# A two-layer decoder trunk: weight loads on ScalarE's DMA queue with three raw buffers, and longer PSUM rings by stage

## The chip, the cores and the metric

The kernel runs on one core of one Trainium2 chip. The metric is the device time in microseconds (us) of one execution of the whole program; lower is better. The core has TensorE (PE, matrix products, results in the banks of PSUM), VectorE (DVE), ScalarE (ACT), GpSimd (POOL) and SyncE (SP), each with its own instruction stream that it works off strictly in order. DMA transfers are issued by an instruction in one of these streams; a DMA instruction that has to wait holds up whatever stands behind it in that stream.

## The reference, cut to what matters

The program is one inference step of a decoder trunk of two layers on 512 prompt tokens and 8 single decode tokens (T = 520 columns). Layer 0 mixes tokens with a gated delta rule (GDN), layer 1 with a Mamba-2 scan (SSD); a gated convolutional feed-forward follows each.

```python
def _conv_ffn(x, buf, w_up, conv_w, conv_b, w_down):
    gv = x @ w_up
    gate, val = gv[..., :D_FF], gv[..., D_FF:]
    gate, new_buf = _causal_dwconv(gate, buf, conv_w, conv_b)
    return (jax.nn.silu(gate) * val) @ w_down, new_buf
...
        if i % N_MIXERS == 0:
            h, nb, ns = _gdn_mixer(...)   # proj, conv, chunked delta rule, gated norm, @ w_out
        else:
            h, nb, ns = _ssd_mixer(...)   # proj, conv, chunked scan, gated norm, @ w_out
        x = _layer_norm(DN_ALPHA * x + h, ln1_g[i], ln1_b[i])
        f, fb = _conv_ffn(x, ffn_conv[i], ffn_w_up[i], ffn_conv_w[i], ffn_conv_b[i], ffn_w_down[i])
        x = _layer_norm(DN_ALPHA * x + f, ln2_g[i], ln2_b[i])
```

D_MODEL is 1024, D_FF 2816. Besides the tokens the outputs hold the new convolution caches and the new states of the mixers: the 8 decode tokens each read, update and write back a state per head, which is most of the DMA traffic that isn't weights.

## The kernel before

Features lie on the 128 partitions, tokens on the free axis, in two halves of HT = 260 columns. All projections are cut into **units**: one block of 128 output features, in one or both halves. There are 252 units and 294 weight **chunks** of up to 8x128x128 float32 values (512 KB). The order of the units is a list (`plan`, L132): the GDN input projection (`gin`), its output projection (`gout`), feed-forward `up0` and `down0`, then `sdt` and `sin`, `sout`, `up1`, `down1`.

**A chunk.** `prep` (L209) takes a tile `raw` (tag "raw", 2 buffers), loads it by a DMA on SP's queue (L215), casts it on ACT to a rounded copy `hi` (L223), and subtracts on DVE or POOL to get the rest `lo` (L224). `hi` and `lo` have 3 buffers each. In `gin` and part of `sin` the subtraction runs on POOL, elsewhere on DVE. `raw` is free for the next chunk when both L223 and L224 are through.

**A unit.** `unit` (L228) takes a PSUM bank per half from `unit_bank` (L117), calls `prep` until two chunks beyond its own are prepared, and for each k of 8 issues three matmuls of 260 columns, hi by XH, hi by XL, lo by XH (L246; `XH`, `XL` are the split activations). Then `evac` empties the bank: in `gin` and `sin` a copy on ACT to `u` (L587, in the program's names `u<-psl`), in `up` a copy on ACT to `u` (L428 for the first half, L442 for the second) for the 22 gate units and a product on DVE to `f` (L481) for the 22 value units, in the output projections a sum on DVE (`R` or `lR`, L308). `f` has 3 buffers, and is split by ACT into `fh` (L278) and by POOL into `fl` (L279).

**Banks.** PSUM has eight banks. In the GDN stage (`self.scan` true) the units turn through the two banks of tag "l"; the other six (A, B, C, D, X, Y) belong to the small matmuls of the chunked delta rule. In every later stage the units turn through three: X, l, l.

**The state updates.** `state` (L978) is called for the decode states, two at a time, from the evacuations of the gate units: an SP load of `Sd` (L984), an SP load of `Sr` (L987), three operations on POOL (L988, L989, L990), and an SP store (L991) that waits for the last of these. `Sd` and `Sr` have 2 buffers. In `up0` there are 16 such updates, in `up1` 32.

**The delta rule.** Per head, `gdn_head` (L736) builds what the chunked rule needs (`kt`, `Kd`, the solve `D`, `X`, `Z`), and `gdn_chunk` (L885) walks the recurrence. The gate units of `gin` (m of 24 and more) write to `z`, a tile of tag "uh" with 2 buffers.

**What sets the order.** The Tile framework's scheduler fixes one order per engine when the program is built, from the order of the code, priorities (`high_priority` around the chunk's load and split) and when buffers come free. On the chip each engine runs its own list in order and waits on semaphores.

Of the kernel before, what the change touches and what calls it, by code (L numbers as in the profile page):

```python
# [9 lines left out]
F32 = mybir.dt.float32  # L10
# [3 lines left out]
ALU = mybir.AluOpType  # L14
# [4 lines left out]
P = 128  # L19
# [3 lines left out]
B = 8  # L23
T = S + B
HT = T // 2
C = 4
# [13 lines left out]
KB = 3  # L40
FF = 2816
# [28 lines left out]
def _bc(ap, dims):  # L70
    return ap.to_broadcast(dims)


class Net:
    def __init__(self, ctx, tc, a):
        self.tc, self.nc, self.a, self.ctx = tc, tc.nc, a, ctx
        nc = self.nc
        pool = lambda name, bufs=1, **k: ctx.enter_context(tc.tile_pool(name=name, bufs=bufs, **k))
        self.const = pool("const")
        self.wp = pool("wp", 3)  # L80
        self.big = pool("big")
# [8 lines left out]
        self.odd, self.scanodd, self.scan, self.nb, self.na = False, False, True, 0, 0  # L90
        self.plan()

    def consts(self):
        nc, a, p = self.nc, self.a, self.const
# [5 lines left out]
        self.halves = p.tile([P, 2, B], F32, name="halves")  # L100
        nc.vector.memset(self.halves[:, 0], -0.5)
        nc.vector.memset(self.halves[:, 1], 0.5)
# [29 lines left out]
    def plan(self):  # L132
# [23 lines left out]
        self.prepped = 0  # L156
# [51 lines left out]

    def prep(self):  # L209
        name, m, k0, kn, i = self.chunks[self.prepped]  # L210
        nc = self.nc
        mw = 64 if name in ("w_gba", "w_sdt") else P
        with self.tc.high_priority():
            raw = self.wp.tile([P, 8, P], F32, tag="raw", name="raw", bufs=2)
            nc.sync.dma_start(out=raw.rearrange("p k m -> p (k m)")[:, :kn * mw], in_=self.a[name][m][:, k0 * mw:(k0 + kn) * mw])  # L215
            raw = raw.rearrange("p k m -> p (k m)")[:, :kn * mw].rearrange("p (k m) -> p k m", m=mw)
# [234 lines left out]
    def ffn(self, l):  # L451
        nc, tc, a = self.nc, self.tc, self.a
        W = 3
        with tc.tile_pool(name=f"ffn{l}", bufs=1) as fp:
            fh = fp.tile([P, KF, T], F32R, name="fh")
            fl = fp.tile([P, KF, T], F32R, name="fl")
            with tc.tile_pool(name=f"up{l}", bufs=1) as p:
# [25 lines left out]

                while self.next_name() == f"up{l}":
                    self.unit(evac)
                nc.sync.dma_start(out=a["o_fconv"][:, l], in_=cout)
# [27 lines left out]
    def softplus(self, pool, z, n, tag):  # L514

        nc = self.nc
        t = {k: pool.tile([P, n], F32, tag=tag + k, name=tag + k) for k in "ewqr"}
        e, w, q, r = (t[k] for k in "ewqr")
# [40 lines left out]
    def gdn(self):  # L559
        nc, tc, a = self.nc, self.tc, self.a  # L560
        W = 4
        with tc.tile_pool(name="gdnr", bufs=1) as rp:
# [6 lines left out]
            with tc.tile_pool(name="gdn", bufs=1) as p:  # L569
# [59 lines left out]
                self.scan = False  # L629
# [106 lines left out]
    def gdn_head(self, p, h, kq, v, decays):  # L736
# [9 lines left out]
        Kd = p.tile([P, C, P], F32, tag="Kd", name="Kd", bufs=4)  # L746
# [54 lines left out]
        tmp = p.tile([P, 2, C, 16], F32, tag="Xtmp", name="Xtmp", bufs=2)  # L801
# [207 lines left out]
    def ssd(self):  # L1009
        nc, tc, a = self.nc, self.tc, self.a  # L1010
        W = 4
        with tc.tile_pool(name="ssdr", bufs=1) as rp:
# [4 lines left out]
            with tc.tile_pool(name="ssd", bufs=1) as p:  # L1017
# [35 lines left out]

                while self.next_name() in ("sdt", "sin"):
                    self.unit(evac)
                nc.sync.dma_start(out=a["o_sconv"], in_=cout)
# [193 lines left out]
    def ssd_norm(self, p, g):  # L1250
# [11 lines left out]
        f = p.tile([P, T], F32, tag="nf", name="nf", bufs=1)  # L1262
# [176 lines left out]
```

## Time and profile before

| | us |
|---|---|
| three runs before | 1784.18, 1792.85, 1791.64 (median 1791.64) |
| the profiled execution: its own time | 1785.41 |
| its span, first to last instruction | 1783.6 |
| PE busy | 1613.7 (90%) |
| DVE busy | 1221.2 (68%) |
| POOL busy | 968.4 (54%) |
| ACT busy | 839.3 (47%) |
| mean granted TensorE clock | 0.973 |

The stages, read from the first matmul of each: `gin` 5 to 384 us, `gout` to 443, `up0` to 723, `down0` to 858.6, the SSD stage (`sdt`, `sin`) to 1238.3, `sout` to 1351, `up1` to 1637, `down1` to 1772, the last layer norm to 1783.6.

A busy PE is a PE with a matmul in its pipeline: successive matmuls of 260 columns overlap, so that a row has 0.28 us although one starts every 0.12 us. What a stage loses is therefore read from the number of matmuls in it against its length. Waits are listed as "who <- whom: total us, times, longest us"; a queue (SPq) is the stream of DMA-issuing instructions of an engine.

### The profile page before, as it was taken

To read this page: it belongs to the slowest core of one execution; us is meant where nothing else is said; L and a number is where in the kernel's file an instruction comes from. 1 tells how busy PE (TensorE), PEld (TensorE's weight loads), DVE (VectorE), ACT (ScalarE), POOL (GpSimd) and SP (SyncE) were. 2 spreads that over 40 slices of the span, in tenths; PEclk is the share of its full clock that TensorE was granted. 3 is DMA by queue.
4 is the path that set the end of the run, shared out by engine and by line. 5 is a ranking of instruction groups with operands and counts; after the bars stand their busy time and mean duration, and the time that the engine had idled before them with its cause. 6 is when DMAs were issued, how large, how long until landed. Compare 5 with 4: busy or idle time off the path is not lost.

```text
span 1783.6 us, 33737 instructions
## 1 busy us (share of the span) xinstructions
PE 1613.7 (90%) x12889; PEld 1550.4 (87%) x12889; DVE 1221.2 (68%) x2133; ACT 839.3 (47%) x1724; POOL 968.4 (54%) x1090
## 2 busy tenths in 40 slices
PE   8888899888999899999888897989988998889997
PEld 7888888888998799998886796979988998889996
DVE  5967888668876544337699989895569765554356
ACT  4644664354563344225665554645236643333134
POOL 4844677655258722215346757676134387876142
PEclk9989999999999999999999999989999999999999
DMA  5422343235466532334644534342564655564334
GB/s 187 131 85 61 103 130 111 86 122 163 146 204 196 171 116 96 88 97 131 188 129 153 163 119 130 125 125 70 160 197 143 209 198 187 190 210 153 96 101 145
DMA packets 108978, 250.36 MB, mean 140 GB/s; under 512 B 15344, under 2 KB 31696, under 8 KB 108784
## 3 DMA queue, kind: packets, MB, share of 16 engines
q1 hardware_dynamic: 108816, 248.20, 44.1%
q8 instruction: 101, 1.65, 0.4%
q14 instruction: 61, 0.50, 0.1%
HBM read 225.80 MB, written 22.92 MB: 139 GB/s over the span
## 4 chain that ended last, share of the span: by engine, by line
PE 30%; DVE 24%; DMA 18%; POOL 14%; ACT 8%; issue 5%; SPq 1%; ACTq 0%; DVEq 0%; POOLq 0%
PE psl L246 26%; DVE lo L224 3%; DMA raw<-w_up 3%; DMA Sr<-bd 3%; POOL Sd L990 3%; ACT hi L223 3%; POOL Sr L988 3%; DVE sE L1180 2%; DMA Sr<-kr 2%; DVE y L419 2%; DMA raw<-w_down 2%; POOL Sd L989 2%; POOL fl L279 1%; DVE Xtmp L812 1%; DMA Sd<-sstate 1%
## 5 line engine op out<-in xcount | busy, mean ns | idle before, releaser
L246 PE MATMUL psl<-XH,hi 128*128 128x260 f32 (+1 forms) x2816 | 819.5, 292 | 61.4 <-ACT u L442 18.4
L246 PE MATMUL psl<-XL,hi 128*128 128x260 f32 (+1 forms) x2848 | 823.6, 290 | 8.8 <-DVE lR L308 3.9
L246 PE MATMUL psl<-XH,lo 128*128 128x260 f32 (+1 forms) x2816 | 809.7, 288 | 2.7 <-DVE lo L224 1.6
L246 PEld LDWEIGHTS psl<-XH,hi 128*128 128x128 f32 (+1 forms) x2816 | 538.9, 192 | 78.0 <-ACT u L442 22.0
L224 DVE TENSOR_TENSOR lo<-raw,hi 128x512 fp32r<-128x512 f32 (+2 forms) x439 | 356.9, 850 | 327.7 <-ACT hi L223 323.3
L246 PEld LDWEIGHTS psl<-XL,hi 128*128 128x128 f32 (+1 forms) x2848 | 545.6, 192 | 15.4 <-issue 5.7
L246 PEld LDWEIGHTS psl<-XH,lo 128*128 128x128 f32 (+1 forms) x2816 | 539.2, 192 | 7.6 <-DVE lo L224 3.1
L223 ACT CAST hi<-raw 128x512 fp32r<-128x512 f32 (+2 forms) x499 | 315.2, 671 | 435.0 <-PE psl L246 191.7
L246 PE MATMUL psl<-fh,lo 128*128 128x260 f32 x704 | 201.2, 286 | 1.8 <-DVE lo L224 1.4
L246 PE MATMUL psl<-fh,hi 128*128 128x260 f32 x704 | 200.3, 284 | 0.7 <-ACT hi L223 0.7
L246 PE MATMUL psl<-fl,hi 128*128 128x260 f32 x704 | 198.8, 282 | 0.0
L224 POOL TENSOR_TENSOR lo<-raw,hi 128x1024 fp32r<-128x1024 f32 x60 | 148.6, 2476 | 53.5 <-ACT hi L223 52.1
L246 PEld LDWEIGHTS psl<-fh,lo 128*128 128x128 f32 x704 | 132.5, 188 | 4.0 <-DVE lo L224 3.6
L246 PEld LDWEIGHTS psl<-fh,hi 128*128 128x128 f32 x704 | 132.5, 188 | 1.4 <-ACT hi L223 0.9
L246 PEld LDWEIGHTS psl<-fl,hi 128*128 128x128 f32 x704 | 132.4, 188 | 0.2
L279 POOL TENSOR_TENSOR fl<-f,fh 128x260 fp32r<-128x260 f32 x88 | 80.3, 914 | 66.4 <-ACT fh L278 66.3
L419 DVE SCALAR_TENSOR_TENSOR s<-u,par,s 128x512 f32<-128x512 f32 x88 | 82.6, 939 | 6.8 <-ACT s L416 6.8
L278 ACT CAST fh<-f 128x260 fp32r<-128x260 f32 x88 | 36.0, 409 | 96.5 <-DVE f L481 96.5
L246 PE MATMUL psl<-y,hi 128*128 128x260 f32 x256 | 73.3, 288 | 1.8 <-DVE y L279 0.8
L990 POOL TENSOR_TENSOR Sd<-Sd,Sr 128x512 f32<-128x512 f32 x48 | 70.1, 1460 | 0.5
L365 POOL TENSOR_TENSOR lnsq<-lnsq,sq 128x260 f32<-128x260 f32 x48 | 46.8, 978 | 28.8 <-ACT sq L363 27.3
L471 POOL COPY cout<-u 128x10 f32<-128x10 f32 x44 | 19.2, 436 | 77.7 <-ACT u L442 77.6
(397 smaller groups left out, 2685.9 us busy)
## 6 DMA issues: line engine op xcount, KB each, us to landing
raw<-w_up SPq DMA_DIRECT2D x106, 512.0 KB
raw<-w_down SPq DMA_DIRECT2D x44, 512.0 KB
raw<-w_sin SPq DMA_DIRECT2D x43, 512.0 KB
raw<-w_gin SPq DMA_DIRECT2D x32, 512.0 KB
Sd<-sstate SPq DMA_DIRECT2D x64, 256.0 KB
raw<-w_down SPq DMA_DIRECT2D x22, 384.0 KB
Sd<-gstate SPq DMA_DIRECT2D x32, 256.0 KB
kb<-kr SPq DMA_DIRECT2D x32, 256.0 KB
```

What stands on the lines that cost most here:

```text
L223: nc.scalar.copy(out=hi[:, ks, :mw], in_=raw[:, ks, :])
L224: eng.tensor_tensor(out=lo[:, ks, :mw], in0=raw[:, ks, :], in1=hi[:, ks, :mw].bitcast(F32), op=ALU.subtract)
L246: self.nc.tensor.matmul(out=ps[h][:mw], lhsT=w[:, b0 + k, :mw], rhs=x[:, hs], start=(k0 + k == first and i == 0), stop=(k0 + k == last and ...
L278: nc.scalar.copy(out=hi, in_=xf)
L279: (eng or nc.gpsimd).tensor_tensor(out=lo, in0=xf, in1=hi.bitcast(F32), op=ALU.subtract)
L365: nc.gpsimd.tensor_tensor(out=acc, in0=acc, in1=sq, op=ALU.add)
L419: nc.vector.scalar_tensor_tensor(out=y[:, :S], in0=u[:, j:j + S], scalar=self.pcol(wname, i * w + j), in1=y[:, :S], op0=ALU.mult, op1=ALU.add)
L471: nc.gpsimd.tensor_copy(out=cout[:, m, :], in_=u[:, 2 + S - 2:2 + T])
L988: nc.gpsimd.tensor_tensor(out=t, in0=t, in1=_bc(col[:, :, None], D4), op=ALU.mult)
L989: nc.gpsimd.tensor_tensor(out=St, in0=St, in1=_bc(decay[:, :, None], D4), op=ALU.mult)
L990: nc.gpsimd.tensor_tensor(out=St, in0=St, in1=t, op=ALU.add)
L1180: nc.vector.tensor_scalar(out=E[:, c, :], in0=E[:, c, :], scalar1=self.acum[:, c, h:h + 1], scalar2=0.0, op0=ALU.subtract, op1=ALU.min)
```

## The change

- `fetch` is new. It takes a `raw` tile (now `RAW` = 3 buffers) and issues its load on ScalarE's queue (`nc.scalar.dma_start`, L223 of the new file; the cast to `hi` is L241 there). `prep` calls it until the chunks up to two beyond the one it prepares are fetched. No weight load is left on SP.
- `unit_bank` turns through a ring that depends on the stage: two banks in the GDN stage (as before), three in the SSD stage (as before), six (X, l, A, Y, l, B) in `gout`, `down0`, `sout`, `down1`, and all eight in `up0` and `up1`.
- SBUF for the third `raw` buffer (4 KB a partition) comes from five places: `halves` has one column per value instead of a filled tile, and is broadcast in `power`; the residual tiles of the layer norms always use tag "u"; `softplus` reuses a tile; `Kd` has 3 buffers instead of 4; `Xtmp` 1 instead of 2; `nf` takes the place of `acc`.

```diff
+    BANKS = {"gdn": "ll", "ssd": "Xll", "out": "XlAYlB", "up": "XlAYlBCD"}
+
     def unit_bank(self):
         self.nb += 1
-        if not self.scan and self.nb % 3 == 1:
-            return self.pss.tile([P, 512], F32, tag="X", name="psl", bufs=1)[:, :HT]
-        return self.psl.tile([P, HT], F32, tag="l", name="psl")
+        tag = self.BANKS[self.stage][self.nb % len(self.BANKS[self.stage])]
+        if tag == "l":
+            return self.psl.tile([P, HT], F32, tag="l", name="psl")
+        return self.pss.tile([P, 512], F32, tag=tag, name="psl", bufs=1)[:, :HT]
...
-    def prep(self):
-        name, m, k0, kn, i = self.chunks[self.prepped]
-        nc = self.nc
+    def fetch(self):
+        name, m, k0, kn, i = self.chunks[self.fetched]
         mw = 64 if name in ("w_gba", "w_sdt") else P
         with self.tc.high_priority():
-            raw = self.wp.tile([P, 8, P], F32, tag="raw", name="raw", bufs=2)
-            nc.sync.dma_start(out=raw.rearrange("p k m -> p (k m)")[:, :kn * mw], in_=...)
-            raw = raw.rearrange("p k m -> p (k m)")[:, :kn * mw].rearrange("p (k m) -> p k m", m=mw)
+            raw = self.wp.tile([P, 8, P], F32, tag="raw", name="raw", bufs=RAW)
+            raw = raw.rearrange("p k m -> p (k m)")[:, :kn * mw]
+            self.nc.scalar.dma_start(out=raw, in_=...)
+        self.raws[self.fetched] = raw.rearrange("p (k m) -> p k m", m=mw)
+        self.fetched += 1
+
+    def prep(self):
+        while self.fetched < min(self.prepped + RAW, len(self.chunks)):
+            self.fetch()
+        ...
+        with self.tc.high_priority():
+            raw = self.raws.pop(self.prepped)
...
     def new_xr(self):
-        if self.lni % 2:
-            return self.lnp.tile([P, HT], F32, tag="xr", name="xr", bufs=4)
         return self.up.tile([P, 3 + T], F32, tag="u", name="xr")[:, :HT]
...
-        self.nc.gpsimd.tensor_tensor(out=y, in0=x, in1=self.halves[:, which, :n], op=ALU.pow)
+        self.nc.gpsimd.tensor_tensor(out=y, in0=x, in1=_bc(self.halves[:, which:which + 1], [P, n]), op=ALU.pow)
...
-        Kd = p.tile([P, C, P], F32, tag="Kd", name="Kd", bufs=4)
+        Kd = p.tile([P, C, P], F32, tag="Kd", name="Kd", bufs=3)
...
-        tmp = p.tile([P, 2, C, 16], F32, tag="Xtmp", name="Xtmp", bufs=2)
+        tmp = p.tile([P, 2, C, 16], F32, tag="Xtmp", name="Xtmp", bufs=1)
```

Three places of the built programs show what moves. The first is SP in the middle of `up1`, where the states are updated; before:

```order
L215 DMA raw<-w_up 128x1024
L984 DMA Sd<-sstate 128x512
L987 DMA Sr<-bd 128x512
L984 DMA Sd<-sstate 128x512
L215 DMA raw<-w_up 128x1024
L991 DMA o_sdec<-Sd 128x512
L987 DMA Sr<-bd 128x512
L991 DMA o_sdec<-Sd 128x512
L215 DMA raw<-w_up 128x1024
```

and after:

```order
L1005 DMA Sr<-bd 128x512
L1002 DMA Sd<-sstate 128x512
L1005 DMA Sr<-bd 128x512
L1002 DMA Sd<-sstate 128x512
L1009 DMA o_sdec<-Sd 128x512 x2
```

The weight loads that stood behind a state store are gone, and the state loads and stores are alone.

The second is ACT in the same stretch; before:

```order
L442 COPY u<-psl 128x260
L416 ACTIVATE s<-u,par 128x520
L278 CAST fh<-f 128x260
L470 ACTIVATE s<-s 128x520
L223 CAST hi<-raw 128x512 x2
L278 CAST fh<-f 128x260
L223 CAST hi<-raw 128x512 x2
```

and after (L458, L432, L296, L486, L241 are the same operations as L442, L416, L278, L470, L223 before; L223 is now the load):

```order
L458 COPY u<-psl 128x260
L432 ACTIVATE s<-u,par 128x520
L223 DMA raw<-w_up 128x1024
L296 CAST fh<-f 128x260
L486 ACTIVATE s<-s 128x520
L241 CAST hi<-raw 128x512 x2
L296 CAST fh<-f 128x260
L223 DMA raw<-w_up 128x1024
L241 CAST hi<-raw 128x512 x2
```

A load now stands one or two ACT instructions behind the cast of the chunk whose buffer it takes, and in front of the next copies; in `gin` and `sin` it stands three to six behind.

The third is PE late in the GDN stage, at the small 32x32 products of the solve (`z`, `xz`); before:

```order
L246 MATMUL psl<-XH,lo 128x260
L847 MATMUL z<-X,M 32x32 x8
L893 MATMUL st<-uo,Kd 128x128
L901 MATMUL o<-Sn,gbc 128x128
L902 MATMUL o<-uo,gbc 128x128
L762 MATMUL kqk<-kq 128x256 x2
L246 MATMUL psl<-XH,hi 128x260
L246 MATMUL psl<-XL,hi 128x260
```

and after, the head of a run that goes on to 27 groups of small matmuls with no unit matmul in between (`psl`); two further runs there have 33 and 21 groups, and the last one 9, where before the four runs have 6, 11, 18 and 9:

```order
L264 MATMUL psl<-XH,lo 128x260
L848 MATMUL z<-X,M 128x64 x4
L780 MATMUL kqk<-kq 128x256 x2
L853 MATMUL xz<-Z_320,XT 128x64 x4
L855 MATMUL xz<-XT,Z_320 128x64 x4
L780 MATMUL kqk<-kq 128x256 x2
L865 MATMUL z<-X,M 32x32 x8
L871 MATMUL xz<-XT,Z_321 32x32 x8
L874 MATMUL xz<-Z_321,XT 32x32 x4
L530 MATMUL qt<-cn,kq 128x128 x4
L881 MATMUL z_2694<-X,M 64x64 x4
L886 MATMUL x_2701<-XT,Z_2699 64x64 x4
```

The order of the units among themselves is the same; small matmuls of the later heads moved towards the end of the stage and stand closer together.

## Rows read from the trace of the kernel before

**Rows 1.** Page, sections 1 and 5: engines' busy time; POOL's subtraction.

```profile
PE 1613.7 (90%) x12889; PEld 1550.4 (87%) x12889; DVE 1221.2 (68%) x2133; ACT 839.3 (47%) x1724; POOL 968.4 (54%) x1090
...
L224 POOL TENSOR_TENSOR lo<-raw,hi 128x1024 fp32r<-128x1024 f32 x60 | 148.6, 2476 | 53.5 <-ACT hi L223 52.1
```

**Rows 2.** Stages: window, length; PE, PEld, DVE, ACT, POOL (counts); clock, DMA.

```profile
5.00:384.00 379.00, 335.45 (x2808) 317.97 (x2809) 282.35 (x647) 191.36 (x523) 239.89 (x277) 0.95 0.36 112
...
443.00:723.00 280.00, 263.45 (x2123) 258.83 (x2122) 170.91 (x259) 131.04 (x265) 135.15 (x177) 0.99 0.47 152
...
858.60:1238.30 379.70, 331.45 (x2501) 306.43 (x2500) 324.89 (x542) 210.47 (x317) 234.08 (x193) 0.96 0.42 134
1238.30:1351.00 112.70, 100.23 (x784) 96.72 (x783) 71.91 (x116) 46.09 (x88) 35.35 (x39) 0.99 0.51 160
1351.00:1637.00 286.00, 264.93 (x2126) 258.88 (x2126) 182.10 (x248) 127.46 (x258) 201.07 (x257) 0.99 0.59 192
```

**Rows 3.** Windows of 50 us, same columns: across down0's start, and in up1.

```profile
700.00:750.00 50.00, 50.00 (x419) 50.00 (x418) 16.26 (x29) 13.05 (x27) 12.78 (x15) 1.00 0.30 88
...
1550.00:1600.00 50.00, 45.29 (x371) 44.41 (x370) 27.58 (x35) 18.72 (x38) 41.88 (x54) 1.00 0.64 202
```

**Rows 4.** Waits in up1: TensorE's weight loads, then ACT's casts.

```profile
PEld psl L246 <- ACT u L442: 15.4, 12, 2.7
PEld psl L246 <- DVE f L481: 5.3, 7, 1.2
PEld psl L246 <- ACT u L428: 4.0, 5, 1.5
...
ACT hi L223 <- DMA raw<-w_up: 86.7, 34, 5.8
```

**Rows 5.** Waits in SP's queue: up1, then the GDN stage.

```profile
SPq L991 <- POOL Sd L990: 82.6, 20, 6.6
...
SPq L215 <- POOL cout L599: 51.5, 11, 8.7
```

**Rows 6.** Timeline in up1, 1477 to 1486 us: one late weight load.

```profile
1477.41 1.29 POOL L990 TENSOR_TENSOR Sd<-Sd,Sr 128x512 f32<-128x512 f32 x1
...
1478.73 0.34 SPq L991 DMA_DIRECT2D o_sdec<-Sd  x1
...
1479.18 0.36 SPq L215 DMA_DIRECT2D raw<-w_up  x1
...
1484.25 1.14 ACT L223 CAST hi<-raw 128x512 fp32r<-128x512 f32 x2 [4.27 <-DMA raw<-w_up]
...
1486.03 0.39 PE L246 MATMUL psl<-XH,hi 128*128 128x260 f32 x1 [1.33 <-ACT u L428]
```

**Rows 7.** Timeline of POOL in up1: a pair of state updates.

```profile
1506.37 1.72 POOL L990 TENSOR_TENSOR Sd<-Sd,Sr 128x512 f32<-128x512 f32 x1
...
1512.84 1.55 POOL L989 TENSOR_TENSOR Sd<-Sd,ddt 128x512 f32<-128x512 f32 x1 [2.07 <-DMA Sd<-sstate]
...
1520.05 1.72 POOL L990 TENSOR_TENSOR Sd<-Sd,Sr 128x512 f32<-128x512 f32 x1
```

**Rows 8.** Waits in up0: TensorE's weight loads.

```profile
PEld psl L246 <- DVE f L481: 5.1, 5, 2.1
PEld psl L246 <- DVE R L308: 5.1, 1, 5.1
PEld psl L246 <- ACT u L442: 4.8, 4, 2.2
PEld psl L246 <- ACT u L428: 3.8, 4, 1.7
```

**Rows 9.** Waits in sout: TensorE's matmuls.

```profile
PE psl L246 <- DVE lR L308: 3.9, 4, 1.5
```

**Rows 10.** GDN stage: a wait of TensorE; a run of 18 small groups.

```profile
PE xz L835 <- DVE Z L832: 3.3, 3, 1.5
...
363.89 0.67 PE L863 MATMUL z<-X,M 64*64 64x64 f32 x8
...
370.70 0.49 PE L893 MATMUL st<-uo,Kd 128*128 128x128 f32 x2 [0.62 <-DVE uo L891]
```

More of the change, by code (lines that the diff above doesn't have):

```diff
@@ L40 @@
 KB = 3
+RAW = 3
 FF = 2816
@@ L90, in __init__ @@
         self.odd, self.scanodd, self.scan, self.nb, self.na = False, False, True, 0, 0
+        self.stage = "gdn"
         self.plan()
@@ L99, in consts @@
         nc.sync.dma_start(out=self.par, in_=a["par"])
-        self.halves = p.tile([P, 2, B], F32, name="halves")
-        nc.vector.memset(self.halves[:, 0], -0.5)
-        nc.vector.memset(self.halves[:, 1], 0.5)
+        self.halves = p.tile([P, 2], F32, name="halves")
+        nc.vector.memset(self.halves[:, :1], -0.5)
+        nc.vector.memset(self.halves[:, 1:], 0.5)
         self.mean = p.tile([P, P], F32, name="mean")
@@ L155, in plan @@
         self.upos = 0
-        self.prepped = 0
+        self.prepped = self.fetched = 0
+        self.raws = {}
         self.ready = {}
@@ L207, in lo_pool @@
         return name in ("gin", "sin") and len(halves) == 2 and (name == "gin" or i % 4 != 3)
+    def fetch(self):
+        name, m, k0, kn, i = self.chunks[self.fetched]
+        mw = 64 if name in ("w_gba", "w_sdt") else P
+        with self.tc.high_priority():
+            raw = self.wp.tile([P, 8, P], F32, tag="raw", name="raw", bufs=RAW)
+            raw = raw.rearrange("p k m -> p (k m)")[:, :kn * mw]
+            self.nc.scalar.dma_start(out=raw, in_=self.a[name][m][:, k0 * mw:(k0 + kn) * mw])
+        self.raws[self.fetched] = raw.rearrange("p (k m) -> p k m", m=mw)
+        self.fetched += 1
     def prep(self):
+        while self.fetched < min(self.prepped + RAW, len(self.chunks)):
+            self.fetch()
         name, m, k0, kn, i = self.chunks[self.prepped]
@@ L213, in prep @@
         with self.tc.high_priority():
-            raw = self.wp.tile([P, 8, P], F32, tag="raw", name="raw", bufs=2)
-            nc.sync.dma_start(out=raw.rearrange("p k m -> p (k m)")[:, :kn * mw], in_=self.a[name][m][:, k0 * mw:(k0 + kn) * mw])
-            raw = raw.rearrange("p k m -> p (k m)")[:, :kn * mw].rearrange("p (k m) -> p k m", m=mw)
+            raw = self.raws.pop(self.prepped)
             hi = self.wp.tile([P, 8, P], F32R, tag="hi", name="hi")
@@ L482, in evac @@
                         self.split(f, fh[:, m, hs], fl[:, m, hs])
+                self.stage = "up"
                 while self.next_name() == f"up{l}":
                     self.unit(evac)
+                self.stage = "out"
                 nc.sync.dma_start(out=a["o_fconv"][:, l], in_=cout)
@@ L516, in softplus @@
         nc = self.nc
-        t = {k: pool.tile([P, n], F32, tag=tag + k, name=tag + k) for k in "ewqr"}
-        e, w, q, r = (t[k] for k in "ewqr")
+        t = {k: pool.tile([P, n], F32, tag=tag + k, name=tag + k) for k in "ewq"}
+        e, w, q, r = (t[k] for k in "ewqe")
         nc.vector.scalar_tensor_tensor(out=w, in0=z, scalar=-1.0, in1=z, op0=ALU.mult, op1=ALU.min)
@@ L628, in gdn @@
                 nc.sync.dma_start(out=a["o_gconv"], in_=cout)
-                self.scan = False
+                self.scan, self.stage = False, "out"
                 def first(name, m, h, ps):
@@ L1052, in evac @@
                             self.ssd_group(p, g, st["B"], st["C"])
+                self.stage = "ssd"
                 while self.next_name() in ("sdt", "sin"):
                     self.unit(evac)
+                self.stage = "out"
                 nc.sync.dma_start(out=a["o_sconv"], in_=cout)
@@ L1261, in ssd_norm @@
                 nc.gpsimd.tensor_tensor(out=acc, in0=acc, in1=sq, op=ALU.add)
-        f = p.tile([P, T], F32, tag="nf", name="nf", bufs=1)
+        f = acc
         for j in range(2):
```

## The prediction

> **What bounds the kernel now.** I read the engines' totals first: PE is busy 90% of the span and nothing else over 68% [rows 1], so a gain has to come out of the tenth in which PE stands, or out of work elsewhere that makes it stand. Then the stages. The pace of PE with nothing in its way is the window across the end of up0 and the start of down0: 419 matmuls in 50 us, 0.1193 us each [rows 3]. By that pace the 2123 matmuls of up0 take 253.3 us and the stage has 280, an excess of 26.7; up1 has 286 - 253.6 = 32.4, sout 112.7 - 93.5 = 19.2 [rows 2]. The granted clock is 0.99 in these, so the excess is waiting. The GDN stage (43.6 us without a PE row) and the SSD stage (48.3) also wait, but there the small matmuls of the recurrences depend on DVE, which is busy 324.9 of the 379.7 us of the SSD stage [rows 2]: that stage has a second floor close to its length.
>
> What the excess of up1 is: weight loads of TensorE wait for a bank, 15.4 us for the copies L442, 5.3 for f, 4.0 for L428, 24.7 together [rows 4]. Why the copies are late is seen on one case [rows 6]: POOL ends a state addition at 1478.70; the store behind it leaves SP at 1478.73; the weight load stands next in SP's queue and leaves at 1479.18; the data come 5 us later; ACT has stood for 4.27 us before the cast at 1484.25, and behind that cast, in ACT's order, stands the copy that frees the bank for which PE waits 1.33 us. ACT waits for weights 86.7 us in up1 in this manner, and SP's stores wait 82.6 us for POOL [rows 4, 5]. So before the change a chain runs from POOL's states through SP to the weights, to ACT, to the bank, to PE.
>
> **The change, term by term,** against the profiled execution's 1785.4 us (the median of the runs shown is 1791.6, 6 us higher; the runs spread over 8.7).
>
> *up1.* No load stands behind a store any more, and eight banks let PE go on over some 2.9 us for each half unit (24 matmuls) that an evacuation is late, against three before. The most to be had is the 24.7 us of bank waits [rows 4]. But a second pace lies under it. A gate unit and its value unit are 4 x 24 matmuls, 11.5 us, and bring two state updates to POOL; POOL has a pair every 13.7 us (L990 at 1506.37 and at 1520.05), and before one of its operations stands 2.07 us for the state's own load [rows 7]. In 1550 to 1600 it is better: PE makes 371 of 419, so a pair takes 11.5 / 0.885 = 12.9 us, and POOL is busy 41.9 of the 50 [rows 3]. POOL also makes fl, in its order behind the states; f has three buffers, fl frees one, and DVE's f frees the bank. So the states can still hold PE by way of f, once the eight banks are full. I take the pair at 12.9, the better stretch that the trace has, since SP will carry the states' loads alone: 16 pairs x 0.8 = 13. **-13**, between -24 (bank waits all gone) and -3 (pair stays at 13.7; only the run-ahead of the longer ring is left, once).
>
> *up0.* Only 8 pairs, and POOL is busy 135 of 280 us [rows 2], so it does not set the pace. Bank waits are 5.1 for f, 4.8 and 3.8 for the copies, 13.7 in all; the 5.1 for R (L308) is the layer norm at the seam and stays [rows 8]. **-12**, between -16 and -5.
>
> *gout, down0, sout, down1.* Six banks instead of three where DVE sums into R: in sout 3.9 us of waits for it [rows 9]; what else is in sout's excess is the chain of the layer norms, which the change doesn't touch. I allow half as much again for the other three: **-6**, between 0 and -10.
>
> *ScalarE's cost.* An issue holds SP 0.36 us [rows 6]; the trace of before has no weight load on ACT, so I take the same: 294 x 0.36 = 106 us more on an engine busy 839 of 1784 [rows 1]; 53 chunks in up1 are 19 us on 127 of 286 [rows 2]. That is covered. Not covered by itself is the wait: a load may leave when the subtraction of the chunk three before is done, and in ACT's order the evacuating copies stand behind it. Such a wait on ACT is bounded by nothing (subtraction long done) and by a whole subtraction, 2.48 us on POOL [rows 1]. In up the load stands one or two instructions behind the cast, so it will wait, but eight banks cover a copy that is 1 or 2 us late. In the GDN and SSD stages there are two and three banks as before, and the load stands three to six instructions behind; so I take it nearer to nothing there.
>
> *The SSD stage.* Same ring, DVE its floor. POOL subtracts 28 chunks here (60 less the 32 of gin): at worst 28 x 2.48 = 69 us of ACT standing, of which a fifth may reach DVE and PE; on the other side the loads no longer stand behind SP's other work. **+2**, between -8 and +15.
>
> *The GDN stage.* Loads are freed from SP's waits for POOL (51.5 us [rows 5]), but PE waits little for weights there, so that is worth a few us at most. Kd with 3 buffers instead of 4 holds back the next head: the order has its small matmuls later and denser, runs of 27, 33, 21 and 9 groups where before there are 6, 11, 18 and 9, 46 more without a unit matmul between them. What such a group costs beyond its work is bounded by two rows: in the run of 18 groups that begins at 363.89 the only idle time is 0.62 us, at 370.70, 0.03 a group, since two heads were interleaved; a bare hop over DVE (xz waiting for Z) is 3.3 / 3 = 1.1 us [rows 10]. 46 groups are 2 us by the one and 51 by the other. The run of 18 is the same sort of work at the same place, so I take nearest to it, with one bare hop at the head of each of the three longer runs (3.3) and a little for ACT's new waits in front of two banks: **+6**, between -10 and +30 as the stage's own part of the range.
>
> *The rest* (halves broadcast, tiles reused, Xtmp with one buffer, nf in acc) puts no instruction more on any engine; nothing waits for them but what is in these stages' bounds.
>
> Sum: -13 - 12 - 6 + 2 + 6 = -23, so 1785.4 - 23 = **1762 us**.
>
> **Rivals.**
> *A, slower: the dense runs are bare.* If the hops of the delta rule's tail cost 1.1 us in each of the 46 groups, the GDN stage is 51 longer instead of 6: 1762 + 45 = 1807. For it speaks that the runs now hold steps of one head that follow on each other (z, xz, z, xz, u, wt, st); against it, that the run of before shows nearly no idle time. It decides from about 0.85 us a group (1801 us).
> *B, no change: the weights were never it.* Then POOL's pair stays at 13.7 us, the casts wait for something else, and the banks alone are worth -3 in up1, -5 in up0, -3 in the output projections; with +2 and +6 this is -3: 1782. The Trainium skill has a rule on this side ("DMA: Bandwidth & Descriptors", section "Issuing engines are not separate DMA queues"): DMAs started by different engines run on the same 16 engines and interleave, so that a second issuing engine saves only the sequencer's issue time. By that rule the move itself is worth nothing here, SP's issue time being on nobody's path. The trace disagrees in one point: the load of [rows 6] was not slow in the DMA engines, it was issued late, behind a store that waited for POOL. The busy share of the DMA engines in up1 is 0.59 [rows 2], and POOL's wait for Sd speaks for B in part.
> *C, more: all bank waits go* (-24, -16, -10), and the GDN and SSD stages gain a little too (-3 together): 1785 - 53 = 1732.
>
> **Chances.** Forecast 0.55 (1745 to 1782), C 0.15, B 0.17, A 0.13. A measurement of this kernel can tell about 0.5%, 9 us, from no change; against the median of 1791.6 that is 1782.7 and 1800.6. Forecast and C are faster: 0.70; B 0.17; A 0.13. The bounds' half widths (10, 5, 5, 11, 20) added as squares give 26; 1.3 times that on either side of 1762, a little less below where C's end already is, is 1730 to 1796, which leaves out half of A and part of C.
>
> **What would show it.** Right: in up1 and up0 ACT's casts no longer wait for the weights' DMA (86.7 us gone), the bank waits on L442, L428 and f fall under 5 us, up1 takes 273 us and up0 268, POOL's pair 12.9. Wrong: f (L481) as the new releaser of PE with POOL's fl behind it and a pair still at 13.7 (B); the GDN stage ending after 405 us with PE standing on Z, XT or uo in the last heads (A); ACT's queue standing at its loads for the subtraction, and PE for u in gin (the term of ScalarE).

## The result, and the profile after

The changed kernel takes 1800.33 us (median of 12 runs, 1794.95 to 1807.45) against 1786.12 for the kernel before in the same measurements; the ratio is 1.0074, with a 95% interval of 1.0053 to 1.0096. It is slower by three quarters of a per cent where a faster kernel, 1762 us, was forecast, and the time lies above the range of 1730 to 1796. Its profiled execution took 1800.73 us. The totals of its page, which answer to [rows 1]:

```profile
span 1798.9 us, 33596 instructions
PE 1624.5 (90%) x12889; PEld 1569.6 (87%) x12889; DVE 1215.8 (68%) x2133; ACT 836.0 (46%) x1724; POOL 962.2 (53%) x1090
```

The windows by stage, columns as in [rows 2]:

```profile
5.00:414.00 409.00, 349.91 (x2804) 329.13 (x2805) 284.24 (x647) 194.39 (x529) 235.96 (x275) 0.91 0.34 103
414.00:477.50 63.50, 55.86 (x417) 54.12 (x415) 54.29 (x98) 32.69 (x72) 35.48 (x42) 0.93 0.50 159
477.50:742.40 264.90, 256.91 (x2120) 255.54 (x2121) 161.75 (x253) 129.02 (x262) 135.09 (x182) 0.98 0.50 158
742.40:873.60 131.20, 129.99 (x1070) 129.01 (x1069) 69.49 (x111) 48.44 (x102) 42.05 (x45) 1.00 0.40 118
873.60:1263.90 390.30, 334.54 (x2505) 312.05 (x2504) 325.08 (x541) 208.52 (x315) 230.84 (x194) 0.94 0.42 130
1263.90:1368.30 104.40, 99.88 (x787) 98.19 (x785) 68.37 (x104) 43.12 (x82) 36.59 (x38) 0.97 0.55 170
1368.30:1654.60 286.30, 265.44 (x2121) 261.14 (x2120) 179.22 (x258) 129.21 (x264) 199.21 (x261) 0.96 0.58 190
1654.60:1787.40 132.80, 131.58 (x1078) 130.38 (x1077) 66.54 (x107) 45.08 (x93) 43.32 (x47) 1.00 0.40 117
```

Held against before: the GDN stage +30 us, gout +4.5, up0 -15, down0 -4, the SSD stage +10.5, sout -8, up1 +0.3, down1 -2. The sum is the +15.3 by which the span grew. So three stages lose 45, four give back 30, and up1, from which the largest gain was forecast, gives nothing.

**The GDN stage.** The windows from the unit matmul before the first dense run (304.6) to the end of the stage, after:

```profile
304.60:331.10 26.50, 19.31 (x149) 16.43 (x148) 19.83 (x56) 11.93 (x32) 17.33 (x19) 0.81 0.26 73
331.10:373.10 42.00, 32.43 (x269) 29.50 (x267) 27.46 (x84) 12.46 (x49) 19.91 (x24) 0.77 0.26 72
373.10:414.00 40.90, 36.60 (x286) 33.84 (x286) 15.88 (x51) 13.14 (x42) 13.74 (x13) 0.83 0.28 78
```

and before, from the same unit matmul on (331.8):

```profile
331.80:355.40 23.60, 19.34 (x171) 18.26 (x170) 16.37 (x46) 7.96 (x25) 15.63 (x17) 0.93 0.35 106
355.40:384.00 28.60, 25.55 (x235) 23.56 (x235) 16.55 (x51) 11.13 (x37) 16.02 (x15) 0.98 0.39 120
```

PE comes to that matmul 27 us earlier than before (the small matmuls that stood ahead of it are now behind it), and needs 109 us from there where it needed 52. PE is busy 88 of these 109 us, but at a granted clock of 0.77 to 0.83. One row of the first dense run, and the same kind of group of before:

```profile
317.35 1.11 PE L886 MATMUL x<-XT,Z 64*64 64x64 f32 x8 [0.46 <-ACT Z L883]
```

```profile
365.14 0.68 PE L868 MATMUL x<-XT,Z 64*64 64x64 f32 x8
```

The first of these stands at the lower of the clock's two levels (1.2 GHz, a granted clock of 0.50), the second at the upper (2.4 GHz):

```profile
316.80:318.80 2.00, 1.54 (x11) 1.33 (x11) 1.86 (x5) 1.14 (x4) 2.00 (x3) 0.50 0.82 224
```

```profile
364.50:366.50 2.00, 2.00 (x20) 1.81 (x19) 1.18 (x4) 1.29 (x6) 1.19 (x1) 1.00 0.18 62
```

By the windows of the whole stage PE has no row for 59.1 us after and for 43.6 before, so 15.5 us of the 30 are additional standing, and the other 14.5 are time in which PE is busy for longer with the same matmuls. The three long dense runs by themselves (27, 33 and 21 groups), and the run of 18 groups of before:

```profile
304.70:330.65 25.95, 18.76 (x144) 15.88 (x143) 19.31 (x53) 11.56 (x32) 17.21 (x18) 0.80 0.26 74
337.58:372.55 34.97, 25.40 (x209) 22.46 (x208) 25.23 (x76) 8.60 (x31) 17.24 (x21) 0.73 0.25 70
384.96:400.48 15.52, 13.28 (x109) 11.91 (x108) 8.53 (x24) 5.65 (x18) 7.54 (x8) 0.70 0.47 137
```

```profile
363.89:371.63 7.74, 7.10 (x61) 6.23 (x60) 4.08 (x12) 4.66 (x15) 5.27 (x5) 1.00 0.47 151
```

In the three runs PE waits 18 times, 19.2 us in all, on steps of the solve and of the recurrence; the longest wait, 4.0 us, is among these of the run of 33:

```profile
PE z L865 <- DVE XT L858: 5.8, 2, 4.0
```

**up1.** The bank waits of [rows 4] are gone: L442 (L458 in the new file), L428 and f release PE no more. ACT's casts, too, wait for the weights' DMA for 2.7 us only, where it was 86.7. In their place, in the waits of up1 after (who waits, for whom: us, times, longest):

```profile
DVE f L497 <- POOL fl L297: 52.3, 13, 7.2
...
PEld psl L264 <- DVE lo L242: 14.9, 9, 5.2
PE psl L264 <- DVE lo L242: 13.0, 9, 5.0
```

PE runs on over eight banks, until the weights themselves are late. Why they are late is seen at 1547 to 1558 us (timeline, start, duration, what was done, idle before and who ended it):

```profile
1547.26 0.82 ACT L432 ACTIVATE s<-u,par 128x520 f32<-128x520 f32 x1
...
1552.21 2.98 POOL L1008 TENSOR_TENSOR Sd<-Sd,Sr 128x512 f32<-128x512 f32 x2
...
1553.98 1.58 SPq L1009 DMA_DIRECT2D o_sdec<-Sd  x2
...
1556.03 0.33 ACTq L223 DMA_DIRECT2D raw<-w_up  x1
...
1556.41 0.41 ACT L296 CAST fh<-f 128x260 fp32r<-128x260 f32 x1 [8.33 <-DMA o_sdec<-Sd]
...
1556.91 0.43 DVE L497 TENSOR_TENSOR f<-s,psl 128x260 f32<-128x260 f32 x1 [4.11 <-POOL fl L297]
...
1557.92 0.39 PE L264 MATMUL psl<-XH,hi 128*128 128x260 f32 x1 [1.89 <-ACT hi L241]
```

ACT is through with L432 at 1548.1 and stands at the weight load until 1556.0, and the trace names what ends it: the transfer of a state store, which SP issued at 1553.98 when POOL was through with its addition. It is the chain of [rows 6] again, though the two transfers are now in different queues. The built program says by which way: its waits name eight completion counters for DMAs (DMAHW0 to 7), which the transfers of both queues share, and a DMA whose counter may still be held by an earlier transfer has to wait for that one. In up1, 39 of the 53 weight loads carry such a wait beside that for DVE:

```
L223 DMA raw_17066<-w_up1 128x1024 [waits DMAHW2_49,DVE_49]
```

The transfer that such a load waits for is another weight load in 22 of the 39, a state's in seven (three stores, two loads of Sd, two of Sr), and one of SP's other tiles in ten. The load of 1556.03 is one of those behind a state store. From the trace, ACT stands 62 us at such counters in the whole program, 26 in up0 and 26 in up1.

There is a second wait in the same rows. DVE works in order, and its product f, ahead of the next lo, stands for POOL's fl: 4.11 us here, 52.3 in up1. fl waits for its own input only 5.3 us in up1; for the rest it stands in POOL's order behind the state operations. In this case lo begins 0.56 us after f; had ACT not stood, DVE's order alone would have let it begin only that much earlier.

### The profile page after: what moved, and what is told of

Its sections match the earlier page's. It is cut to its first block, busy times and chain, and to the rows that moved or that the text cites. A ratio compares the mean times of both kernels' runs of the same rounds, so it can differ in the third digit from the quotient of the medians.

```text
span 1798.9 us, 33596 instructions
## 1 busy us (share of the span) xinstructions
PE 1624.5 (90%) x12889; PEld 1569.6 (87%) x12889; DVE 1215.8 (68%) x2133; ACT 836.0 (46%) x1724; POOL 962.2 (53%) x1090
## 5 line engine op out<-in xcount | busy, mean ns | idle before, releaser
L264 PE MATMUL psl<-XH,lo 128*128 128x260 f32 (+1 forms) x2816 | 819.4, 292 | 17.0 <-DVE lo L242 17.0
L264 PEld LDWEIGHTS psl<-XH,hi 128*128 128x128 f32 (+1 forms) x2816 | 545.9, 194 | 33.9 <-ACT u L605 12.4
L264 PEld LDWEIGHTS psl<-XH,lo 128*128 128x128 f32 (+1 forms) x2816 | 545.3, 194 | 24.4 <-DVE lo L242 19.7
L242 DVE TENSOR_TENSOR lo<-raw,hi 128x512 fp32r<-128x512 f32 (+2 forms) x439 | 345.6, 824 | 240.9 <-ACT hi L241 235.0
L241 ACT CAST hi<-raw 128x512 fp32r<-128x512 f32 (+2 forms) x499 | 313.7, 669 | 327.8 <-PE psl L264 252.5
L297 POOL TENSOR_TENSOR fl<-f,fh 128x260 fp32r<-128x260 f32 x88 | 76.5, 871 | 51.5 <-ACT fh L296 51.5
L296 ACT CAST fh<-f 128x260 fp32r<-128x260 f32 x88 | 35.9, 408 | 143.3 <-DVE f L497 130.9
L497 DVE TENSOR_TENSOR f<-s,psl 128x260 f32<-128x260 f32 x88 | 36.7, 419 | 90.3 <-POOL fl L297 61.4
L435 DVE SCALAR_TENSOR_TENSOR s<-u,par,s 128x512 f32<-128x512 f32 x88 | 88.1, 1001 | 9.0 <-ACT s L432 8.2
L1200 DVE TENSOR_SCALAR sE<-sE,acum 128x128 f32<-128x128 f32 x128 | 65.7, 572 | 2.6 <-DMA sE<-ad 2.6
```

Source lines behind the costliest of these rows:

```text
L241: nc.scalar.copy(out=hi[:, ks, :mw], in_=raw[:, ks, :])
L242: eng.tensor_tensor(out=lo[:, ks, :mw], in0=raw[:, ks, :], in1=hi[:, ks, :mw].bitcast(F32), op=ALU.subtract)
L264: self.nc.tensor.matmul(out=ps[h][:mw], lhsT=w[:, b0 + k, :mw], rhs=x[:, hs], start=(k0 + k == first and i == 0), stop=(k0 + k == last and ...
L296: nc.scalar.copy(out=hi, in_=xf)
L297: (eng or nc.gpsimd).tensor_tensor(out=lo, in0=xf, in1=hi.bitcast(F32), op=ALU.subtract)
L435: nc.vector.scalar_tensor_tensor(out=y[:, :S], in0=u[:, j:j + S], scalar=self.pcol(wname, i * w + j), in1=y[:, :S], op0=ALU.mult, op1=ALU.add)
```

## The experiments

All stage lengths come from one profiled execution each: the GDN stage and sout run to the first unit matmul of the next stage, down1 to PE's last row, the others from their first unit matmul to their last. Kd is not used in up1, and yet up1 has 285.5 us before and 289.7 in e1, where Kd alone is changed: differences of up to some 4 us in a stage tell nothing. "Pair" is the mean distance of POOL's state additions, two by two, in up1: 13.5 us before, 13.4 after.

**Kd alone, and everything but Kd.** The first run does only this to the kernel before:

```diff
-        Kd = p.tile([P, C, P], F32, tag="Kd", name="Kd", bufs=4)
+        Kd = p.tile([P, C, P], F32, tag="Kd", name="Kd", bufs=3)
```

> The kernel before with one edit: Kd has 3 buffers instead of 4. Theory K (the third Kd buffer alone reorders the tail of the GDN stage into dense runs): the GDN stage takes about 405 us instead of 379 (the changed kernel has 408), every other stage stays as before, the whole is 20 to 30 us slower than before (about 1810). Rival Q (the GDN stage is longer because ScalarE issues and waits for the loads): the GDN stage stays at 379 +- 4 and the time is that of before within 0.3%.

1822.5 us, ratio 1.019 (1.0158 to 1.0222). The GDN stage:

```profile
5.00:416.00 411.00, 346.86 (x2789) 329.50 (x2790) 288.63 (x660) 190.79 (x520) 239.56 (x278) 0.89 0.33 104
```

The second gives Kd its fourth buffer back in the changed kernel (`Kd` bufs=4, `RAW = 2` to make room).

> The changed kernel with Kd at 4 buffers again, paid for with two raw buffers instead of three; loads still on ScalarE, rings as changed. Theory K: the GDN stage falls to 380 to 388 us, the rest stays as in the changed kernel if the third raw buffer is worth little: about 1775. Rival Q: the GDN stage stays at 400 or more (ScalarE's waits are longer with two buffers), the time is 1800 or more.

1791.0, ratio 1.0025 (1.0007 to 1.0042). The GDN stage:

```profile
5.00:384.50 379.50, 336.94 (x2804) 318.52 (x2805) 289.15 (x647) 190.26 (x527) 239.29 (x275) 0.95 0.35 110
```

Theory K holds from both sides: one buffer less of one tile is worth the whole 30 us of this stage, and ScalarE's queue costs it nothing. The total of the second run was missed by 16, since up1 grew to 297 and down1 to 139 with two raw buffers. In up1 ACT stands only 1.2 us at counters there, but DVE's f stands for fl even longer than in the changed kernel:

```profile
1345.90:1643.10 297.20, 270.66 (x2122) 265.00 (x2123) 168.71 (x254) 128.56 (x259) 198.67 (x263) 0.95 0.57 184
...
DVE f L497 <- POOL fl L297: 81.6, 17, 8.9
```

So with two raw buffers up1 is long almost without the counters.

**The ring without the queue, the queue without the ring, three buffers without the queue.** e3 is the kernel before with `BANKS`; e4 the changed kernel with `"out": "Xll", "up": "Xll"`; e7 the changed kernel with `self.nc.sync.dma_start` in `fetch`.

> The kernel before with the longer rings alone: loads on SP, two raw buffers, Kd at 4. If the rings are what made up0, down0, sout and down1 shorter in the changed kernel (theory R): up0 about 266 us, sout 104, down0 131, the GDN stage 379 as before, up1 286, together about 1755 to 1762. If it was the queue (rival W): up0 stays at 275 to 280, sout at 110 or more, and the time is 1780 or more.

> The changed kernel with the old ring (X, l, l) in all stages after the GDN stage: loads on ScalarE with three raw buffers, Kd at 3. Theory R: the GDN stage stays at 408, up0 goes back to 275 to 280 us, sout to 110, the time is about 1820. Rival W (the queue made the gain): up0 stays at 265 to 268 and sout at 105, the time is about 1800.

> The changed kernel with the weight loads back on SP's queue; three raw buffers, rings and Kd as changed. If ScalarE's queue made the SSD stage longer (390 in the changed kernel, 377 to 380 in the three kernels with loads on SP): SSD 376 to 381. The GDN stage stays near 405 (Kd at 3), up0 at 270 to 275 (with the ring alone 275, with the queue too 265), the time about 1795. Rival: the SSD stage stays at 385 to 390, then its length comes from the order that the third raw buffer brings.

Ratios 1.002 (1.0001 to 1.0039), 1.0096 (1.0065 to 1.0126), 0.9996 (0.9983 to 1.0009). The stages:

| us | before | ring (e3) | queue, 3 raw (e4) | ring, 3 raw on SP (e7) | all (after) |
|---|---|---|---|---|---|
| up0 | 279.8 | 275.2 | 272.6 | 268.0 | 264.8 |
| down0 | 135.5 | 136.4 | 131.5 | 130.6 | 131.1 |
| SSD | 379.6 | 376.5 | 384.6 | 376.4 | 390.2 |
| sout | 113.0 | 107.0 | 107.5 | 103.1 | 104.3 |
| up1 | 285.5 | 294.0 | 288.7 | 289.5 | 286.4 |

Neither theory R nor W is right alone. up0 gains 5 us from the ring alone, 12 with the third raw buffer besides (e7), 13 with ScalarE's queue besides and two buffers (e2, 266.7), 15 with all three; the shorter down0 comes with the third raw buffer; sout is shortened by either. e7 differs from the changed kernel in the queue alone: its ratio is 0.9996 against 1.0074, so the move to ScalarE by itself costs some 14 us, and the SSD stage has 13.8 of them. Its length goes with ScalarE's queue throughout: 383 to 395 us in all eleven kernels that have it, 375 to 380 in all nine with the loads on SP. PE's largest additional wait there is at `yo`, in the changed kernel:

```profile
PE yo L1210 <- DVE Sn L1187: 16.1, 3, 6.9
```

8.0 us before, and 6.6 in e7, with ring and buffers but the loads on SP. By which steps ScalarE's loads delay that sum, no run here has taken apart. In e7 gout ends at 481 us, in the changed kernel at 477.5, where before it ended at 443: Kd has 3 buffers in both. And no kernel of the three made up1 shorter.

**What holds up1.** Four edits of the changed kernel: fl on DVE (e5), no states in up1 (e6), three buffers for the states (e9), both of e5 and e9 (e10).

```diff
-                        self.split(f, fh[:, m, hs], fl[:, m, hs])
+                        self.split(f, fh[:, m, hs], fl[:, m, hs], nc.vector)
...
-                                    if self.later:
+                                    if l == 0 and self.later:
...
-        St = p.tile(D4, F32, tag="Sd", name="Sd", bufs=2)
+        St = p.tile(D4, F32, tag="Sd", name="Sd", bufs=3)
...
-        t = p.tile(D4, F32, tag="Sr", name="Sr", bufs=2)
+        t = p.tile(D4, F32, tag="Sr", name="Sr", bufs=3)
```

> The changed kernel with one edit: in up0 and up1 the low part fl of f is subtracted on DVE instead of POOL (44 operations of about 0.9 us off POOL in each stage). In the changed kernel a pair of state updates takes POOL 13.4 us in up1 (13.5 before), and DVE's f waits 52 us for fl. Theory P (POOL's stream sets up1's pace, and fl ties PE to it through f): up1 falls from 286 to 258 to 268 us, the wait of f for fl is gone, the time is about 1777. Rival S (the states' loads and stores set the pace by themselves, or DVE's new work takes it back): up1 stays at 280 or more.

Ratio 1.0052 (1.0034 to 1.007). up1 is 283.7 us, the pair 13.5: that POOL's busy time sets the pair falls, since 1.8 us of its work a pair less left the pair where it was. That fl ties PE to POOL does not fall with it, for ACT's standing at counters in up1 grew from 26 to 46 us at the same time. Its largest piece is at the end of up1:

```profile
1628.45 0.33 SPq L1002 DMA_DIRECT2D Sd<-sstate  x1
...
1631.93 0.34 ACTq L223 DMA_DIRECT2D raw<-w_down  x1
1632.31 0.41 ACT L296 CAST fh<-f 128x260 fp32r<-128x260 f32 x1 [25.66 <-DMA Sd<-sstate]
...
1633.29 0.58 PE L264 MATMUL psl<-XH,hi 128*128 128x260 f32 x1 [12.43 <-ACT hi L241]
```

ACT stands 25 us at one weight load, for the counter of a state's load, which itself came behind the stores. PE stands 12.4 for it; without this one stand up1 would have 271 us (283.7 - 12.4, an estimate).

> The changed kernel without the 32 state updates of up1 (their loads, POOL operations and stores are left out, so those outputs are missing). Theory P: up1 falls to 256 to 262 us, its matmuls at their own pace plus the seam. Rival: if the rings or ScalarE's waits at the loads hold up1, it stays above 275.

A single run, 1783.9 us. Without the states up1 is 20 us shorter, a little more than the theory's 262:

```profile
1371.30:1637.70 266.40, 260.43 (x2121) 258.21 (x2120) 139.80 (x260) 132.49 (x265) 66.78 (x103) 0.97 0.36 113
```

So it is the states, and not the ring or ScalarE's issuing. By which of the two waits they hold up1, for the counters or for fl, this run doesn't tell, since both are gone.

> The changed kernel with 3 buffers instead of 2 for each of the state tiles Sd and Sr of up0 and up1. A pair of updates took 13.4 to 13.5 us in up1 in the kernel before, in the changed one, and also when fl was taken off POOL, so theory P (POOL's busy time) is down. Theory S (the round trip of the state's own two buffers sets it: store, its landing, load, three operations): with a third buffer the next load starts earlier, the pair falls to 11.5 to 12.3 us, up1 to 268 to 274. Rival L (the pair is slow because transfers of both queues wait for each other's completion counters): the pair stays at 13.2 or more and up1 above 280.

> The changed kernel with both: fl on DVE and 3 buffers for Sd and Sr. Theory S with POOL at 11.5 us a pair as the next bound: this falls below that of the kernel with three state buffers alone, pair about 11.5, up1 265 to 268, and the time is about 1778. Rival L: up1 stays above 278.

Ratios 1.0013 (0.9994 to 1.0032) and 1.0012 (0.9991 to 1.0032). up1 277.3 and 275.2, pair 12.7 and 12.9, ACT's standing at counters 31 us in each instead of 62; in e10 20 of them are one standing at the end. Between the two theories: the round trip is part of it, but the pair hardly follows. e9 leaves fl on POOL, and DVE's f stands 21 us for it there.

**The states off the counters.** In e13 the changed kernel's `state` issues its transfers on POOL, where they have counters of their own; e14 does it with fl on DVE and three state buffers.

```diff
-        nc.sync.dma_start(out=St, in_=src)
+        nc.gpsimd.dma_start(out=St, in_=src)
```

(and so for the other two transfers of `state`).

> The changed kernel with the states' loads and stores (up0, up1) issued by POOL instead of SP, where they use other completion counters than the weight loads on ScalarE: of the 53 weight loads of up1, 39 wait for a counter in the changed kernel, 11 here. Theory L (a weight load on ScalarE stands for the counter that an SP transfer of a state still holds, and so behind a store that waits for POOL): ScalarE's standing at counters in up0 and up1 (26 us each in the changed kernel, the longest 8 us) falls under 8 us each, and TensorE's waits for hi and lo in up1 (about 16 us) with it, unless POOL's issuing makes the pair itself longer than 13.4 us. Theory S alone: the standing goes, but up1 stays at 283 to 290, since the pair still takes 13.4 us.

> As the run before it, with fl on DVE and 3 buffers for Sd and Sr, so that POOL has room for issuing; to be held against the kernel with fl and 3 buffers alone (up1 275 us, one standing of 20 us at a counter). Theory L: that standing goes, up1 is 268 to 272. Rival (POOL's issuing costs as much as it frees): up1 275 or more.

Ratios 1.0081 (1.0055 to 1.0108) and 0.9974 (0.9954 to 0.9995). In e13, up1 and down1:

```profile
1364.60:1635.90 271.30, 261.30 (x2121) 258.87 (x2120) 195.68 (x258) 128.97 (x264) 193.41 (x286) 0.97 0.54 177
1636.00:1791.30 155.30, 133.96 (x1078) 132.50 (x1076) 71.36 (x106) 44.94 (x94) 94.11 (x119) 0.93 0.45 141
```

ACT's standing at counters in up0 and up1 is nil, and up1 is 15 us shorter although the pair has grown to 17.1 us (POOL now spends 0.54 us on each issue). This decides against S as the bound: the states may be slow, as long as the weights don't wait for them. For theory L e13 is no clean proof, since DVE's standing for fl, 52.3 us in the changed kernel, went with it:

```profile
DVE f L497 <- POOL fl L297: 3.6, 3, 2.6
```

But what POOL doesn't get done in up1 it does in down1, where the residual of the layer norm (`xr`, made on POOL) stands behind the states and PE waits for the first sum:

```profile
PE psl L264 <- DVE R L347: 19.8, 1, 19.8
```

up1 and down1 together are 427 us, 419 in the changed kernel. In e14, where POOL has less to do, the debt is not there:

```profile
1369.70:1636.50 266.80, 260.83 (x2121) 258.61 (x2120) 230.90 (x297) 128.71 (x263) 189.45 (x283) 0.97 0.60 192
1636.60:1769.60 133.00, 131.45 (x1077) 130.22 (x1076) 76.11 (x112) 45.33 (x94) 65.61 (x78) 1.00 0.47 139
```

That is the length of up1 without states; 27 of the 32 additions are made by its end, and the other five cost down1 nothing. Here the counters can be told apart: e10 and e14 both have fl on DVE and three state buffers, and differ in the queue of the states alone. In e10 ACT stands 20 us once,

```profile
ACT fh L296 <- DMA Sr<-bd: 20.6, 1, 20.6
```

in e14 never, and up1 falls from 275.2 to 266.8. So theory L is shown for these 8 us. How the 20 us between the changed kernel and e14 divide between the counters and fl beyond that, no run tells: none takes the one wait away and leaves the other as it is in the changed kernel.

**Put together.** e8 and e12 add to the ring alone (loads on SP, two raw buffers, Kd at 4) fl on DVE, and then 4 state buffers; e15 and e16 have the 4 state buffers without ring and fl, and with the ring; e17 is e12 with the states on POOL; e11 and e18 are e12 and e17 with the loads on ScalarE.

> The kernel before with the longer rings, and fl on DVE in up0 and up1; loads on SP with two raw buffers, Kd at 4. Theory P: up1, 294 us with the rings alone, falls to 265 to 272, up0 to 265 to 270, the GDN stage 378, the SSD stage 377: about 1755 to 1765. Rival S: up1 stays above 285, the time is that of before within 0.5%.

> The loads on ScalarE's queue with two raw buffers, Kd at 4, the longer rings, fl on DVE, 4 buffers for Sd and Sr. Theory S and K together: GDN stage 378 us, up0 262 to 267, SSD 385, sout 104, up1 266 to 272: about 1760. Rival L: up1 stays at 290 or more (297 with two raw buffers so far).

> The kernel before with the longer rings, fl on DVE and 4 buffers for Sd and Sr; loads on SP with two raw buffers, Kd at 4. Theory S: up1, 284 us without the state buffers, falls to 266 to 272; GDN 379, SSD 379, up0 268 to 275: about 1758. Rival L: up1 stays above 280, about 1772.

> The kernel before with 4 buffers for Sd and Sr and nothing else. Theory S: the pair falls from 13.5 to 12.6 us or less and up1 from 286 to 273 to 278 even with the old ring; the rest as before: about 1775. Rival (the ring is needed for it): up1 stays above 282.

> The kernel before with the longer rings and 4 buffers for Sd and Sr, fl on POOL as before. Theory S: up1 falls from the ring's 294 to 278 to 282; against the kernel that also has fl on DVE (278) it shows what fl is worth: about 1760 to 1765. Rival: up1 stays at 288 or more, then fl was the larger part.

> The kernel of e12 (before, with the longer rings, fl on DVE, 4 buffers for Sd and Sr) with the states' loads and stores issued by POOL. The weight loads then share SP's queue in up0 and up1 with no state transfer, neither in order nor by a counter. Theory L (in-order form of it on SP): up1 falls from 278 to 266 to 270 us, up0 from 268 to 264 to 267, the rest as in e12; about 1746. Rival: the ring's remaining waits are those of two raw buffers, then up1 stays at 275 or more.

> The kernel of e11 (loads on ScalarE with two raw buffers, Kd at 4, longer rings, fl on DVE, 4 state buffers) with the states' transfers issued by POOL. Theory L: up1 falls from 280 to 266 to 270, the standing of 24 us at a counter is gone; GDN 376, SSD 386 as in all kernels with loads on ScalarE; about 1757. Against the run beside it this tells what ScalarE's queue is worth when nothing of the states stands in the way of either: theory: nothing, or a loss of 8 to 10 in the SSD stage.

| | median us | ratio (95%) | GDN | up0 | SSD | up1 | down1 |
|---|---|---|---|---|---|---|---|
| e8 ring, fl | 1776.0 | 0.9926 (0.9911 to 0.9941) | 380.4 | 275.2 | 379.4 | 284.0 | 136.4 |
| e15 bufs 4 | 1777.0 | 0.9921 (0.9891 to 0.995) | 381.6 | 272.7 | 378.1 | 281.8 | 136.1 |
| e16 ring, bufs 4 | 1777.9 | 0.9935 (0.991 to 0.9961) | 377.9 | 268.8 | 376.2 | 288.3 | 137.2 |
| e12 ring, fl, bufs 4 | 1756.5 | 0.986 (0.9834 to 0.9886) | 377.6 | 267.8 | 376.6 | 278.1 | 136.2 |
| e17 as e12, states on POOL | 1767.7 | 0.9883 (0.9843 to 0.9923) | 378.9 | 269.7 | 375.2 | 270.5 | 139.5 |
| e11 as e12, loads on ScalarE | 1774.4 | 0.996 (0.9942 to 0.9978) | 375.4 | 264.9 | 385.8 | 280.5 | 138.9 |
| e18 as e17, loads on ScalarE | 1783.4 | 0.9971 (0.9948 to 0.9993) | 379.1 | 269.9 | 383.5 | 282.5 | 139.6 |

The best is e12, 1.4% faster than before, with every load left on SP. Six of the seven expectations of up1 were too low, by 4 to 13 us against their upper ends: in e12 the pair is 12.4 and the loads still stand in SP's order among the states. In e16 the rival came true (288.3), so that fl was the larger part there: with the ring and the loads on SP, fl on DVE is worth 10 us of up1 both without the four state buffers (e3 to e8) and with them (e16 to e12), and the buffers 6. e17 brought up1 where theory L put it (270.5), but PE then stands 8 us at the seam to down1 for POOL's states, so the whole is no better. e18 missed: no standing at counters in up0 and up1, fl on DVE, and up1 still 282.5. Between it and e14 (266.8) lie the third raw buffer, the state buffers (3 there, 4 here) and Kd, which is not used in up1; ACT waits 18 us for the weights' DMA in e18 and not in e14. So I put most of the 16 us down to the raw buffer; a run with that difference alone was not made. Against e12, ScalarE's queue (e11) costs 9 us in the SSD stage and gains 3 in up0.

## Why the prediction was wrong

- **The GDN stage, +6 forecast, +30 measured: the step that failed.** The order was read rightly (46 more groups in dense runs, from Kd), and the place and the sign too; what failed is the price of a group, taken at 0.03 us from the run of 18 in [rows 10] with three bare hops added. The size of a bare hop was right, 1.07 us (19.2 / 18) against 1.1; but there were 18 of them in the three long runs and not three. With 15.5 us more standing a group costs 0.3 us, between the two rows. As much again, 14.5 us, is PE busy for longer, for which the sum had no term: the granted clock is 0.70 to 0.80 in the dense runs and 1.00 in the run of 18, and the same products take longer at the lower level. How much of the 14.5 is the clock and how much is lost overlap with unit matmuls, no run tells apart. The run of 18 stands so little with two heads in turn; the run of 27 and the first half of the run of 33 follow one head's solve, with only the next head's preparation between. That is a part of the reason only, for in the second half of the run of 33 two heads alternate as well, and it still stands 4.0 us. The bound of +30 was just reached.
- **Rival A** named the place and the sign, but that its 1807 lies near the 1800 measured is luck: at 1.1 us in all 46 groups it has the GDN stage at +51, where +30 was measured and only half of it was standing, and what it had too much there is made up by up1 and the SSD stage, which came out 13 and 8.5 us worse than it took them. Its threshold was added up wrongly, too: 0.85 us a group gives 1795, and 1801 needs 0.98. The two ends of that one cost were 49 us apart, more than twice the whole forecast gain, and the likelier value was chosen by likeness of the work, not by counting in the order which group needs the result of the one just before.
- **up1, -13 forecast, +0.3 measured, outside the bounds of -24 to -3.** The first half was right: the waits of [rows 4] for banks are gone, and the chain from the states to the weights in [rows 6] was the real one. Two steps failed. The one is "no load stands behind a store any more": in order it doesn't, through the completion counters it does, for 26 us of ACT's standing. The other is the way by f, which the prediction saw, but took for slack at a pair of 12.9: the pair stayed at 13.4, and DVE's f stands 52 us for fl, ahead of lo. That is the sign set down for rival B in part, with lo and not f as PE's releaser. With both waits gone (e13, e14) up1 has the 15 to 20 us that the ring alone couldn't give. The pair as such is no pace: in e13 up1 is shorter with a pair of 17.1.
- **The Trainium skill's rule in rival B** (a second issuing engine saves only issue time) was nearer to up1 than the forecast, though for another reason: the DMA engines are busy 0.58 of up1 after and 0.59 before, and it was a wait in front of the transfer that tied the queues together. In the whole the move to ScalarE was worth less than nothing: against e7 it costs some 14 us. As a sum B said 1782 with the GDN stage at +6.
- **up0** -12 forecast, -15 measured; **the output projections** -6 forecast, -10.4 measured with gout's +4.5 in it. The mechanism was not only the ring: down0 took its 4 us from the third raw buffer.
- **The SSD stage** +2 forecast, +10.5 measured, inside its bounds of -8 to +15; that it comes with ScalarE's queue the runs show, by which steps they don't.
- **ScalarE's cost** as such was rightly put at nothing for the issues (0.33 us each); its standing at the loads was bounded by one subtraction, 2.48 us. Standings of 6 to 8 us happened, and 25 in e5: the bound left out that a load can wait for something else than its buffer.

## What to carry to other kernels

When SBUF is found by taking a buffer from a tile of a serial chain, count in the built order how many steps now follow on the step that they need: 30 us went with one buffer of Kd, as much as all else gained. The standing was only half of that here, for TensorE's clock was lower in the same stretches. Moving DMAs to another engine's queue takes them out of one order of waiting only; look in the built program for what else the transfer waits for, here a completion counter shared with the very stores it was to get away from. When a run takes away the wait that a theory names, look whether another wait went with it. And where two bounds of one cost lie further apart than the forecast gain, that cost is the prediction; decide it by dependence, not by likeness.

## What was not expected of the hardware

In the dense runs of small, dependent matmuls, in which PE stood 19 of 76 us, the granted clock of TensorE had a mean of 0.70 to 0.80 of full speed, part of the time at its level of 1.2 GHz and part at 2.4; the same group of eight 64x64 products took 1.11 us at the lower level and 0.68 at the upper. And an issue of a state's load from POOL took 0.54 us (e13) where one from SP took 0.33 to 0.42 and a weight load on ScalarE 0.33.
